# Seven products for eight on part of two more projections, their sums halved in two operations

## The chip, the core and the metric

The kernel runs on one core of a Trainium2 chip. TensorE (PE in the profile) multiplies, VectorE (DVE) and ScalarE (ACT) do elementwise work, GpSimd (POOL) a few small steps, and SyncE (SP) issues the loads. What is measured is the device time of one execution in microseconds (us).

## The reference

One decoder layer: 256 tokens, a model width of 2048, everything in float32.

```python
h = rms_norm(x, norm_g)
q, k, v, z_a, u_b, v_b, z_b, g_a, g_b = split(h @ w_in)   # seven of 1024 columns, two of 2048
att = moba_attention(rms_norm(q), rms_norm(k), v)         # 8 heads of 128
y_a = (att * silu(z_a)) @ w_proj_a                        # 1024 -> 2048
y_b = (spatial_gating(gelu(u_b), gelu(v_b)) * silu(z_b)) @ w_proj_b
merged = sigmoid(g_a) * y_a + sigmoid(g_b) * y_b
return x + merged @ w_out                                 # 2048 -> 2048
```

## The kernel before

**Units.** All weights are laid out on the host as a stream of 120 blocks of 128 x 2048 words (1 MB). Block i is a unit: one load into `raw{i}`, one preparation, one group of matmuls. The order of the units is that of `schedule()`: q (units 0 to 7), k (8 to 15), v, za, vb, ub and zb (48 to 55) of eight units each, then four times eight units of the gates (g0 to g3) followed by four of the two branch projections (`proj`), and last 16 units of the output projection (104 to 119). The eight units of a stage are the eight pairs kp = 0 to 7 of the contraction: each holds rows k and k + 8 (of 16 blocks of 128) for two blocks of 512 columns, so four blocks W11, W12, W21, W22.

**Float32 by halves.** Each operand is cast to a shorter format (h) on ACT, and what the cast lost (l) is subtracted out on DVE (`halve`). A product is then three matmuls, l x h, h x h and h x l (`three`): in a unit done directly, `wh` is the cast of the block and `wl` the rest.

**Eight products or seven.** A unit done directly (`direct`) takes eight products, 24 matmuls of 128 x 512. A unit with kp in `SK` that is not of q takes seven (`seven`, Winograd's form of Strassen's scheme), 21 matmuls, and is here called a seven unit. It needs four sums of weight blocks (`t`, three DVE operations), the halves of three blocks (`whp`, `wlp`, 1536 wide) and of the four sums (`th`, `tl`, 2048 wide), and forms of the other operand (`forms`, `halves_f`), made once. Its products go to three banks of PSUM that the direct units share (`L`) and four banks of their own (`E`). After the last seven unit of a stage `early` takes the E banks out, and after the last unit `final` adds the L banks.

**Buffers and order.** `raw` and `t` share four buffers, `wh` with `th` three, `wl` with `tl` three, `whp` and `wlp` two each. The preparation of unit i + 2 and the load of unit i + 3 are written at unit i, and a scheduler sets the order on each engine once the q stage is through. Every engine runs its instructions in that order. A table (`at`) adds the rest of the layer at given units; `turn_m` transposes column block c of the merged result (two transposes of four blocks into PSUM, then its halves) for the output projection, which is done directly, row by row of its columns (`mm_rows`, then `post_out`).

Of the kernel before, what the change touches and what calls it, by code (L numbers as in the profile page):

```python
# [46 lines left out]
def schedule():  # L47
    s = []

    def quad(name, c, order):  # L50
        s.extend(("quad", name, c, kp, n) for n, kp in enumerate(order))

    quad("q", 0, PLAIN)
    for name in ("k", "v", "za", "vb", "ub", "zb"):
        quad(name, 0, MIXED)
    for c in range(4):
        quad("g", c, MIXED)
        s.extend(("proj", "proj", c, q, q) for q in range(4))
    for c in range(4):
        s.extend(("out", "out", c, q, q) for q in range(4))  # L60
    return s
# [3 lines left out]
def hybrid_layer_kernel(  # L65
# [57 lines left out]
    def split(i, pieces=1, js=None):  # L123
# [119 lines left out]
    Fs, Fh, Fl = None, None, None  # L243
# [39 lines left out]
    def direct(L, hs, ls, i, kp, start, stop):  # L283
# [5 lines left out]
        for c, kh in order:  # L289
# [4 lines left out]
            three(L[c], hi, lo, wh[i][:, o:o + B], wl[i][:, o:o + B], start and kh == 0, stop and kh == 1,  # L294
                  first=(i == 0))

    def seven(E, L, i, kp, first, last, started):
# [3 lines left out]
        def A(kh, r):  # L301
            return xh[0][:, a + kh, r * P:(r + 1) * P], xl[0][:, a + kh, r * P:(r + 1) * P]

        def Fm(n):
            return Fh[:, n, kp % 4, :], Fl[:, n, kp % 4, :]
# [14 lines left out]
    def early(E, name):  # L320
# [160 lines left out]
    def turn_m(c, banks):  # L481
        t = slot(F32R, f"mT{c}").rearrange("p (a k t) -> p a k t", a=2, t=S)
        X["mT", c] = t
        for m in range(2):
            ps = transpose4(banks[m], X["m", c][m], f"ps_mT{c}{m}")
            halves(t[:, 0, :, m * P:(m + 1) * P], t[:, 1, :, m * P:(m + 1) * P], ps)
# [23 lines left out]
    def load_res(c):  # L510
        for m in range(2):
            xres[c, m] = u(f"xres{c}{m}")
            nc.scalar.dma_start(xres[c, m], x[m * P:(m + 1) * P, c * B:(c + 1) * B])

    def post_out(c, m, acc):
        o = xres[c, m]
        pieces = 2 if (c, m) == (3, 1) else 1
        n = B // pieces
        for a in range(pieces):
            sl = slice(a * n, (a + 1) * n)  # L520
            nc.vector.tensor_tensor(o[:, sl], acc[:, sl], o[:, sl], op=ALU.add)
            nc.sync.dma_start(out[m * P:(m + 1) * P, c * B + a * n:c * B + (a + 1) * n], o[:, sl])
# [72 lines left out]
    for kp in range(1, 4):  # L595
        split_x(kp)
        if kp < 2:
            split(kp, 4)
    E, L = [0, 2, 4, 3], [1, 5, 6, 7]
    e = None  # L600
    for i, (kind, name, c, kp, n) in enumerate(G):
# [8 lines left out]
        if kind == "quad":  # L610
            if n == 0:
# [7 lines left out]
            if kp in SK and not plain:
                seven(Et, Lt, i, kp, kp == SK[0], kp == SK[-1], n > 0)  # L620
                if kp == SK[-1]:
                    e = early(Et, f"{name}{c}")
            else:
                direct(Lt, xu_h if plain else xh, xu_l if plain else xl, i, kp, n == 0, n == 7)
# [100 lines left out]
```

## Time and profile before

| | |
|---|---|
| median of 3 runs | 681.86 us (681.32 to 682.17) |
| the profiled execution | 681.6 us, of which 679.8 us are the span of the profile |
| PE busy | 663.5 us (98%), 3018 matmuls and transposes |
| DVE busy | 554.6 us (82%) |
| ACT busy | 390.7 us (57%) |
| DMA | 135.31 MB, 199 GB/s |

Busy shares are means over stages that differ: the stage windows and the waits show where an engine is short. A matmul's duration in the profile overlaps the next one's; the distance of their starts is what one costs.

### The profile page before, as it was taken

The numbers are of one execution on the slowest core, as the hardware profiler recorded it, in microseconds if no ns is written. First come the engines' busy times: TensorE is split into PE (matmuls) and PEld (weight loads), VectorE is DVE, ScalarE is ACT, GpSimd is POOL, SyncE is SP. The second block draws the span as 40 slices with busy tenths as digits, with TensorE's granted clock in tenths as the row PEclk, the third lists the DMA queues.
The fourth block names the chain that finished last, engine by engine and source line by source line (L and its number), as shares of the span: only waits on it lengthen the run. The fifth ranks groups of instructions, "written<-read, shape, count | busy, mean of one in ns | idle before, by whom it ended". The sixth has DMA issues, their size and how long they took to land.

```text
span 679.8 us, 7696 instructions
## 1 busy us (share of the span) xinstructions
PE 663.5 (98%) x3018; PEld 544.1 (80%) x3018; DVE 554.6 (82%) x504; ACT 390.7 (57%) x459; POOL 33.3 (5%) x28
## 2 busy tenths in 40 slices
PE   8899999999999999999989999999999999999997
PEld 4677778788788887887877888888888888888886
DVE  4499988899999899998998988978879886654551
ACT  7777867766873685675545834654554555333330
POOL 1001203000010008000000000000000000000000
PEclk9999999999999999999999999999999999999999
DMA  8972573454444624734555725935763475846610
GB/s 305 419 254 79 185 272 142 153 239 168 193 166 186 245 74 177 288 132 161 224 182 224 275 75 200 338 129 185 269 227 124 186 287 211 272 179 235 232 39 31
DMA packets 21923, 135.31 MB, mean 199 GB/s; under 512 B 2432, under 2 KB 3072, under 8 KB 6656
## 3 DMA queue, kind: packets, MB, share of 16 engines
q1 hardware_dynamic: 20736, 132.73, 53.0%
q10 hardware_dynamic: 1152, 2.10, 1.2%
q8 instruction: 23, 0.38, 0.2%
q14 instruction: 12, 0.10, 0.0%
HBM read 132.72 MB, written 2.10 MB: 198 GB/s over the span
## 4 chain that ended last, share of the span: by engine, by line
PE 73%; DVE 12%; issue 4%; DMA 4%; ACT 4%; POOL 0%; SPq 0%; DVEq 0%; ACTq 0%
PE acc_g L279 14%; PE y L279 13%; PE acc_out L279 13%; PE seven_g L279 5%; PE acc_ub L279 4%; PE acc_za L279 4%; DMA raw<-in_w 4%; PE acc_vb L279 4%; DVE wl L121 3%; PE acc_v L279 2%; PE acc_zb L279 2%; DVE wlp L121 2%; ACT th L120 2%; DVE tl L121 2%; PE seven_za L279 2%
## 5 line engine op out<-in xcount | busy, mean ns | idle before, releaser
L121 DVE TENSOR_TENSOR wl<-raw,wh 128x2048 fp32r<-128x2048 f32 (+2 forms) x87 | 183.1, 2115 | 65.3 <-ACT wh L120 64.8
L120 ACT CAST wh<-raw 128x2048 fp32r<-128x2048 f32 (+2 forms) x87 | 153.7, 1774 | 103.3 <-PE acc_out L279 45.7
L120 ACT CAST th<-t 128x2048 fp32r<-128x2048 f32 x40 | 76.5, 1912 | 102.6 <-DVE t L141 102.6
L121 DVE TENSOR_TENSOR tl<-t,th 128x2048 fp32r<-128x2048 f32 x40 | 92.0, 2300 | 28.3 <-ACT th L120 27.7
L279 PE MATMUL acc_out<-wh,mT 128*128 128x512 f32 x256 | 79.0, 390 | 0.0
L120 ACT CAST whp<-raw 128x1536 fp32r<-128x1536 f32 x40 | 59.2, 1481 | 30.5 <-DMA raw<-in_w 16.1
L121 DVE TENSOR_TENSOR wlp<-raw,whp 128x1536 fp32r<-128x1536 f32 x40 | 70.0, 1751 | 0.5 <-ACT whp L120 0.5
L279 PEld LDWEIGHTS acc_out<-wh,mT 128*128 128x128 f32 x256 | 47.9, 188 | 9.8
L279 PE MATMUL acc_g<-wh,xh 128*128 128x512 f32 x128 | 49.8, 389 | 0.0
L279 PE MATMUL acc_out<-wl,mT 128*128 128x512 f32 x128 | 49.8, 389 | 0.0
L279 PE MATMUL acc_g<-wh,xl 128*128 128x512 f32 x128 | 49.7, 389 | 0.0
L138 DVE TENSOR_TENSOR t<-raw 128x1024 f32<-128x1024 f32 x40 | 48.8, 1219 | 0.6
L279 PE MATMUL acc_g<-wl,xh 128*128 128x512 f32 x128 | 48.9, 389 | 0.0
L229 POOL TENSOR_TENSOR rs<-ms,mhalf 128x4 f32<-128x4 f32 x12 | 25.8, 2171 | 126.2 <-DVE ms L228 126.2
L279 PE MATMUL acc_q<-wl,xuh 128*128 128x512 f32 x64 | 25.5, 399 | 3.1 <-DVE wl L121 2.9
L279 PEld LDWEIGHTS acc_g<-wl,xh 128*128 128x128 f32 x128 | 24.0, 188 | 5.2
L279 PEld LDWEIGHTS acc_g<-wh,xl 128*128 128x128 f32 x128 | 24.0, 188 | 5.0
L279 PEld LDWEIGHTS acc_out<-wl,mT 128*128 128x128 f32 x128 | 24.0, 188 | 5.0
L140 DVE TENSOR_TENSOR t<-t,raw 128x512 f32<-128x512 f32 x40 | 27.7, 693 | 0.3
L279 PEld LDWEIGHTS acc_g<-wh,xh 128*128 128x128 f32 x128 | 24.0, 188 | 5.0
L141 DVE TENSOR_TENSOR t<-t,raw 128x512 f32<-128x512 f32 x40 | 27.4, 684 | 0.3
L279 PE MATMUL acc_q<-wh,xuh 128*128 128x512 f32 x64 | 25.1, 392 | 1.6 <-ACT wh L120 1.6
(453 smaller groups left out, 1430.3 us busy)
## 6 DMA issues: line engine op xcount, KB each, us to landing
raw<-in_w SPq DMA_DIRECT2D x117, 1024.0 KB, 4.9
raw<-in_w SPq DMA_DIRECT2D x5, 512.0 KB, 7.4
xnat<-in_x SPq DMA_DIRECT2D x2, 1024.0 KB, 12.7
xres<-in_x ACTq DMA_DIRECT2D x8, 256.0 KB, 6.1
out<-xres SPq DMA_DIRECT2D x7, 256.0 KB, 4.6
xt<-in_xT SPq DMA_DIRECT2D x3, 512.0 KB, 9.6
raw<-in_w SPq DMA_DIRECT2D x2, 256.0 KB, 4.7
ws<-in_wsT SPq DMA_DIRECT2D x2, 256.0 KB, 3.0
```

What stands on the lines that cost most here:

```text
L120: nc.scalar.copy(h, r)
L121: nc.vector.tensor_tensor(l, r, f(h), op=ALU.subtract)
L138: nc.vector.tensor_tensor(two, r[:, B:3 * B].rearrange("p (a n) -> p a n", a=2), r[:, None, 0:B].to_broadcast([P, 2, B]), op=ALU.add)
L140: nc.vector.tensor_tensor(t[:, 2 * B:3 * B], t[:, 0:B], r[:, 2 * B:3 * B], op=ALU.add)
L141: nc.vector.tensor_tensor(t[:, 3 * B:], t[:, 2 * B:3 * B], r[:, 3 * B:], op=ALU.add)
L229: nc.gpsimd.tensor_tensor(dst, ms[:, :n], mhalf[:, :n], op=ALU.pow)
L279: nc.tensor.matmul(acc, a, b, start=(start and n == 0), stop=(stop and n == 2))
```

## The change

Four things change.

- Each of the four gate stages does a fifth pair, kp = 4, with seven products (5 of 8). The forms for this pair are 128 wide (`forms_4`), and their halves are put into columns of `xh[0]` and `xl[0]` that no seven unit reads (`halves_4`). The order of the pairs becomes `GATE`.
- The output projection becomes two stages of eight pairs (out0 and out1, 1024 columns each) with pairs 0 to 3 in seven products. The merged result is kept in float32 too (`mf`), its forms are made while the last branch projection runs (`forms`, `halves_f` with "m"), and `turn_m` 2 comes ahead of 1. The residual x is added in `early` instead of at the end.
- The halves of the four sums are made in two operations each on ACT and DVE (columns 0 to 1023, then the rest), and the casts stand ahead of the subtractions.
- The seven products come in the order W21, W22, W11, sums 0, 1, 2, 3. Before it was W21, W22, sum 3, W11, sums 2, 1, 0.

```diff
+GATE = (5, 0, 1, 6, 2, 3, 4, 7)
+OUT = ((0, 1, 4, 2, 5, 3, 6, 7), (4, 0, 1, 5, 2, 3, 6, 7))
...
-        quad("g", c, MIXED)
+        quad("g", c, GATE)
...
-    for c in range(4):
-        s.extend(("out", "out", c, q, q) for q in range(4))
+    for c in range(2):
+        quad("out", c, OUT[c])
...
+        return G[i][3] in SK or (G[i][1] == "g" and G[i][3] == 4)
...
-        halve(wh[i], wl[i], r[:, B:])
...
-        halve(th[i], tl[i], t)
+        a, b = slice(0, 2 * B), slice(2 * B, WORDS)
+        nc.scalar.copy(wh[i], r[:, B:])
+        for sl in (a, b):
+            nc.scalar.copy(th[i][:, sl], t[:, sl])
+        nc.vector.tensor_tensor(wl[i], r[:, B:], f(wh[i]), op=ALU.subtract)
+        for sl in (a, b):
+            nc.vector.tensor_tensor(tl[i][:, sl], t[:, sl], f(th[i][:, sl]), op=ALU.subtract)
...
-        for acc, (hi, lo), (bh, bl) in ((L[0], A(1, 0), W("21")), (L[1], Fm(3), W("22")), (L[2], A(1, 1), T(3))):
-            three(acc, hi, lo, bh, bl, not started, False)
-        for acc, (hi, lo), (bh, bl) in ((E[0], A(0, 0), W("11")), (E[1], Fm(1), T(2)), (E[2], Fm(2), T(1)),
-                                       (E[3], Fm(0), T(0))):
-            three(acc, hi, lo, bh, bl, first, last)
+        for acc, (hi, lo), (bh, bl) in ((L[0], A(1, 0), W("21")), (L[1], Fm(3), W("22")), (E[0], A(0, 0), W("11")),
+                                       (E[3], Fm(0), T(0)), (E[2], Fm(2), T(1)), (E[1], Fm(1), T(2)),
+                                       (L[2], A(1, 1), T(3))):
+            three(acc, hi, lo, bh, bl, first if any(acc is e for e in E) else not started, last and any(acc is e for e in E))
...
+        if res:
+            for t, r, op in ((c11, res[0], ALU.add), (c12, res[1], ALU.subtract), (h, res[2], ALU.add),
+                             (c22, res[3], ALU.subtract)):
+                nc.vector.tensor_tensor(t, t, r, op=op)
...
+    at(i0 + 4, forms_4)
+    at(i0 + 5, lambda: forms(xt[0], "x"))
...
+    at(i0 + 20, halves_4)
...
-    at(first["proj", 3] + 1, turn_m, 1, "L23")
-    at(first["proj", 3] + 3, turn_m, 2, "L23")
-    at(first["out", 0] + 1, turn_m, 3, "L23")
-    for c in range(4):
-        at(first["out", 0] + 4 * c - 2, load_res, c)
+    at(first["proj", 3] + 1, turn_m, 2, "L23")
+    at(first["proj", 3] + 2, lambda: forms(X["mf", 0], "m"))
+    at(first["proj", 3] + 2, halves_f, "m")
+    at(first["proj", 3] + 2, turn_m, 1, "L01")
+    at(first["out", 0] + 0, turn_m, 3, "L3")
+    at(first["out", 0] + 0, load_res, 0)
+    at(first["out", 1] - 1, load_res, 1)
```

What this does to the order of the engines, at three places. First PE in a seven unit of the gates (g1; `xh`, `xl`, `Fh`, `Fl` are the other operand's halves). Before, unit 70 up to the first matmul that reads `tl`:

```order
L279 MATMUL acc_g1_0_3093<-whp70_3085,xl0_419 128x512
L279 MATMUL acc_g1_0_3093<-whp70_3085,xh0_418 128x512
L279 MATMUL acc_g1_0_3093<-wlp70_3086,xh0_418 128x512
L279 MATMUL acc_g1_1_3094<-whp70_3085,Fl_423 128x512
L279 MATMUL acc_g1_1_3094<-whp70_3085,Fh_422 128x512
L279 MATMUL acc_g1_1_3094<-wlp70_3086,Fh_422 128x512
L279 MATMUL acc_g1_2_3095<-th70_3089,xl0_419 128x512
L279 MATMUL acc_g1_2_3095<-th70_3089,xh0_418 128x512
L279 MATMUL acc_g1_2_3095<-tl70_3090,xh0_418 128x512
```

Now, unit 72 up to the same point:

```order
L303 MATMUL acc_g1_0_3175<-whp72_3240,xl0_424 128x512
L303 MATMUL acc_g1_0_3175<-whp72_3240,xh0_423 128x512
L303 MATMUL acc_g1_0_3175<-wlp72_3241,xh0_423 128x512
L303 MATMUL acc_g1_1_3176<-whp72_3240,Flx_428 128x512
L303 MATMUL acc_g1_1_3176<-whp72_3240,Fhx_427 128x512
L303 MATMUL acc_g1_1_3176<-wlp72_3241,Fhx_427 128x512
L303 MATMUL seven_g1_0_3209<-whp72_3240,xl0_424 128x512
L303 MATMUL seven_g1_0_3209<-whp72_3240,xh0_423 128x512
L303 MATMUL seven_g1_0_3209<-wlp72_3241,xh0_423 128x512
L303 MATMUL seven_g1_3_3212<-th72_3242,Flx_428 128x512
L303 MATMUL seven_g1_3_3212<-th72_3242,Fhx_427 128x512
L303 MATMUL seven_g1_3_3212<-tl72_3243,Fhx_427 128x512
```

The first use of the low half of the sums moves from the ninth matmul to the twelfth, and only its first 1024 columns are read there; the last columns are first read by the 18th.

Second DVE near the end of g0 (units 61 to 63; `t` sums, `wlp` and `tl` low halves). Before, where 61 and 62 are the last two seven units of the stage:

```order
L121 TENSOR_TENSOR wl60_2713<-raw60_2668,wh60_2712 128x2048
L138 TENSOR_TENSOR t61_2747<-raw61_2710 128x1024
L121 TENSOR_TENSOR wlp61_2752<-raw61_2710,whp61_2751 128x1536
L140 TENSOR_TENSOR t61_2747<-t61_2747,raw61_2710 128x512
L121 TENSOR_TENSOR wlp62_2787<-raw62_2745,whp62_2786 128x1536
L141 TENSOR_TENSOR t61_2747<-t61_2747,raw61_2710 128x512
L138 TENSOR_TENSOR t62_2782<-raw62_2745 128x1024
L140 TENSOR_TENSOR t62_2782<-t62_2782,raw62_2745 128x512
L121 TENSOR_TENSOR tl61_2756<-t61_2747,th61_2755 128x2048
L141 TENSOR_TENSOR t62_2782<-t62_2782,raw62_2745 128x512
L121 TENSOR_TENSOR tl62_2791<-t62_2782,th62_2790 128x2048
L121 TENSOR_TENSOR wl63_2821<-raw63_2780,wh63_2820 128x2048
```

Now, where they are the last two of three in a row (60 precedes them in the same form):

```order
L143 TENSOR_TENSOR t61_2813<-raw61_2770 128x1024
L155 TENSOR_TENSOR wlp61_2818<-raw61_2770,whp61_2817 128x1536
L145 TENSOR_TENSOR t61_2813<-t61_2813,raw61_2770 128x512
L157 TENSOR_TENSOR tl61_2820<-t61_2813,th61_2819 128x1024
L146 TENSOR_TENSOR t61_2813<-t61_2813,raw61_2770 128x512
L155 TENSOR_TENSOR wlp62_2858<-raw62_2811,whp62_2857 128x1536
L157 TENSOR_TENSOR tl61_2820<-t61_2813,th61_2819 128x1024
L143 TENSOR_TENSOR t62_2853<-raw62_2811 128x1024
L145 TENSOR_TENSOR t62_2853<-t62_2853,raw62_2811 128x512
L146 TENSOR_TENSOR t62_2853<-t62_2853,raw62_2811 128x512
L157 TENSOR_TENSOR tl62_2860<-t62_2853,th62_2859 128x1024
L126 TENSOR_TENSOR wl63_2891<-raw63_2851,wh63_2890 128x2048
```

Each `tl` stands in two pieces, the first of them right behind the second sum and not behind the third; the last piece of `tl62` follows `wl63`.

Third DVE between the last branch projection (units 100 to 103) and the output projection (`ps_mT` transposed blocks, `g3` the last gate, `y` the branch projections). Before:

```order
L121 TENSOR_TENSOR wl104_4289<-raw104_4226,wh104_4288 128x2048
L471 TENSOR_TENSOR mT0_4256<-ps_mT00_4257,mT0_4256 128x4x128
L471 TENSOR_TENSOR mT0_4256<-ps_mT01_4264,mT0_4256 128x4x128
L471 TENSOR_TENSOR mT1_4271<-ps_mT10_4272,mT1_4271 128x4x128
L471 TENSOR_TENSOR mT1_4271<-ps_mT11_4279,mT1_4271 128x4x128
L121 TENSOR_TENSOR wl105_4325<-raw105_4286,wh105_4324 128x2048
L494 TENSOR_TENSOR g3_c12_4150<-y2_30_4292,g3_c12_4150 128x512
L494 TENSOR_TENSOR g3_c22_4149<-y2_31_4293,g3_c22_4149 128x512
L495 TENSOR_TENSOR g3_c11_4147<-g3_c11_4147,g3_c12_4150 128x512
L495 TENSOR_TENSOR g3_h_4148<-g3_h_4148,g3_c22_4149 128x512
L121 TENSOR_TENSOR wl106_4376<-raw106_4322,wh106_4375 128x2048
```

Now, from the third form of the merged result on:

```order
L289 TENSOR_TENSOR Fm_4446<-mf0_4373,Fm_4446 128x512
L145 TENSOR_TENSOR t105_4473<-t105_4473,raw105_4404 128x512
L157 TENSOR_TENSOR tl105_4480<-t105_4473,th105_4479 128x1024
L146 TENSOR_TENSOR t105_4473<-t105_4473,raw105_4404 128x512
L531 TENSOR_TENSOR g3_c11_4262<-y0_30_4315,g3_c11_4262 128x512
L295 TENSOR_TENSOR Flm_4452<-Fm_4446,Fhm_4451 128x2048
L502 TENSOR_TENSOR ml1_4456<-ps_mT10_4457,mh1_4455 128x4x128
L502 TENSOR_TENSOR ml1_4456<-ps_mT11_4464,mh1_4455 128x4x128
L157 TENSOR_TENSOR tl105_4480<-t105_4473,th105_4479 128x1024
L531 TENSOR_TENSOR g3_h_4263<-y0_31_4316,g3_h_4263 128x512
L533 TENSOR_TENSOR g3_c12_4265<-y2_30_4420,g3_c12_4265 128x512
L533 TENSOR_TENSOR g3_c22_4264<-y2_31_4421,g3_c22_4264 128x512
```

Ahead of the last two merges there now stand the sums and the low halves of units 104 and 105, the forms of the merged result and their low half `Flm`; before there stood two `wl`.

## Rows read from the trace of the kernel before

**Rows 1.** The page: busy time by engine, then the clock in 40 slices.

```profile
PE 663.5 (98%) x3018; PEld 544.1 (80%) x3018; DVE 554.6 (82%) x504; ACT 390.7 (57%) x459; POOL 33.3 (5%) x28
...
PEclk9999999999999999999999999999999999999999
```

**Rows 2.** Chain that ended last, in order of time: start, us, what.

```profile
563.65 10.88 PE y L279 x48
574.53 1.75 PE ps_mT L376 x16
...
587.22 0.87 PE ps_mT L376 x8
...
676.05 0.02 issue
```

**Rows 3.** Stage windows: v, zb, g0, g2, its projection, the last projection, output projection.

```profile
core 0: us, PE busy (x) PEld busy (x) DVE busy (x) ACT busy (x) POOL busy (x), PEclk, DMA share, GB/s
99.16:143.23 44.07, 43.20 (x198) 35.23 (x196) 38.63 (x37) 33.76 (x66) 6.21 (x7) 1.00 0.52 191
283.60:328.84 45.24, 44.73 (x213) 37.19 (x212) 41.53 (x37) 28.66 (x34) 0.00 (x0) 1.00 0.50 191
328.84:374.14 45.30, 41.99 (x182) 33.61 (x181) 41.62 (x37) 24.12 (x19) 0.00 (x0) 1.00 0.50 184
460.29:501.09 40.80, 40.80 (x182) 33.80 (x181) 35.26 (x31) 19.56 (x13) 0.00 (x0) 1.00 0.59 229
501.09:522.85 21.76, 21.76 (x98) 18.02 (x97) 17.32 (x14) 11.95 (x9) 0.00 (x0) 1.00 0.43 148
563.65:588.09 24.44, 24.44 (x122) 20.55 (x121) 15.70 (x16) 12.09 (x12) 0.00 (x0) 1.00 0.71 226
588.09:676.05 87.96, 87.95 (x392) 72.58 (x391) 40.26 (x27) 27.64 (x18) 0.00 (x0) 1.00 0.46 161
```

**Rows 4.** PE in time, in v and in g0: start, us, [idle before <- what ended it].

```profile
118.42 0.39 PE L279 MATMUL seven_v<-whp,xl 128*128 128x512 f32 x1
119.67 0.50 PE L279 MATMUL acc_v<-tl,xh 128*128 128x512 f32 x1 [0.87 <-DVE tl L121]
...
365.60 0.50 PE L279 MATMUL acc_g<-th,xl 128*128 128x512 f32 x1 [1.40 <-ACT th L120]
```

**Rows 5.** DVE in time, zb and g0, columns as in group 4.

```profile
289.22 1.21 DVE L138 TENSOR_TENSOR t<-raw 128x1024 f32<-128x1024 f32 x1
290.36 1.75 DVE L121 TENSOR_TENSOR wlp<-raw,whp 128x1536 fp32r<-128x1536 f32 x1
292.02 0.68 DVE L140 TENSOR_TENSOR t<-t,raw 128x512 f32<-128x512 f32 x1
292.63 1.75 DVE L121 TENSOR_TENSOR wlp<-raw,whp 128x1536 fp32r<-128x1536 f32 x1
...
303.36 2.29 DVE L121 TENSOR_TENSOR tl<-t,th 128x2048 fp32r<-128x2048 f32 x1 [1.43 <-ACT th L120]
...
365.57 2.29 DVE L121 TENSOR_TENSOR tl<-t,th 128x2048 fp32r<-128x2048 f32 x1 [2.02 <-ACT th L120]
367.78 2.29 DVE L121 TENSOR_TENSOR wl<-raw,wh 128x2048 fp32r<-128x2048 f32 x1
...
564.21 0.68 DVE L335 TENSOR_TENSOR g_c<-acc_g,g_c 128x512 f32<-128x512 f32 x1
```

**Rows 6.** Groups by form: busy, mean ns of one, idle before.

```profile
L365 DVE SCALAR_TENSOR_TENSOR vb_c<-vb_c,rs,gain 128x128 f32<-128x128 f32 x12 | 3.3, 345 | 0.0
L470 ACT CAST mT<-ps_mT 128x512 fp32r<-128x512 f32 x8 | 4.2, 593 | 0.0
L120 ACT CAST wh<-raw 128x1024 fp32r<-128x1024 f32 x2 | 2.0, 1047 | 0.0
L120 ACT CAST th<-t 128x2048 fp32r<-128x2048 f32 x40 | 76.5, 1912 | 102.6 <-DVE t L141 102.6
```

**Rows 7.** Loads by line: KB each, median us from issue to landing.

```profile
raw<-in_w SPq DMA_DIRECT2D x117, 1024.0 KB, 4.9
```

More of the change, by code (lines that the diff above doesn't have):

```diff
@@ L293, in direct, with seven @@
             o = BLK[f"{kh + 1}{col + 1}"] * B
-            three(L[c], hi, lo, wh[i][:, o:o + B], wl[i][:, o:o + B], start and kh == 0, stop and kh == 1,
+            three(L[c], hi, lo, wh[i][:, o:o + B], wl[i][:, o:o + B], start[c == 3] and kh == 0, stop and kh == 1,
                   first=(i == 0))
-    def seven(E, L, i, kp, first, last, started):
+    def seven(E, L, i, kp, first, last, started, hs, ls, Fh, Fl):
         a = 2 * (kp % 4)
         def A(kh, r):
-            return xh[0][:, a + kh, r * P:(r + 1) * P], xl[0][:, a + kh, r * P:(r + 1) * P]
+            return hs[kp // 4][:, a + kh, r * P:(r + 1) * P], ls[kp // 4][:, a + kh, r * P:(r + 1) * P]
         def Fm(n):
-            return Fh[:, n, kp % 4, :], Fl[:, n, kp % 4, :]
+            if kp == 4:
+                return spare(hs[0])[:, n], spare(ls[0])[:, n]
+            return Fh[:, n, kp, :], Fl[:, n, kp, :]
         def W(b):
@@ L481, in turn_m @@
     def turn_m(c, banks):
-        t = slot(F32R, f"mT{c}").rearrange("p (a k t) -> p a k t", a=2, t=S)
-        X["mT", c] = t
+        i = c % 2
+        for a in ("mh", "ml") + (("mf",) if i == 0 else ()):
+            if (a, i) not in X:
+                X[a, i] = slot(F32 if a == "mf" else F32R, f"{a}{i}").rearrange("p (k t) -> p k t", t=S)
         for m in range(2):
-            ps = transpose4(banks[m], X["m", c][m], f"ps_mT{c}{m}")
-            halves(t[:, 0, :, m * P:(m + 1) * P], t[:, 1, :, m * P:(m + 1) * P], ps)
+            ps = transpose4(banks[m % len(banks)], X["m", c][m], f"ps_mT{c}{m}")
+            d = (slice(None), slice(c // 2, 8, 2), slice(m * P, (m + 1) * P))
+            if i == 0:
+                nc.scalar.copy(X["mf", i][d], ps)
+            if i == 0 and c == 0 and m == 1:
+                continue
+            halves(X["mh", i][d], X["ml", i][d], ps)
     def merge(c, Y):
@@ L510, in load_res, with post_out @@
     def load_res(c):
[L511 to L522, printed above, removed]
+        xres[c] = [u(f"xres{c}{j}") for j in range(4)]
+        for j, t in enumerate(xres[c]):
+            m, o = j // 2, (2 * c + j % 2) * B
+            nc.scalar.dma_start(t, x[m * P:(m + 1) * P, o:o + B])
+    def post_out(c, L, e):
+        for j in range(4):
+            m, o = j // 2, (2 * c + j % 2) * B
+            pieces = 2 if (c, j) == (1, 3) else 1
+            n = B // pieces
+            for a in range(pieces):
+                sl = slice(a * n, (a + 1) * n)
+                final_one(L, e, j, sl)
+                nc.sync.dma_start(out[m * P:(m + 1) * P, o + a * n:o + (a + 1) * n], e[j][:, sl])
     first = {}
@@ L598, in hybrid_layer_kernel, with fac, direct22 @@
             split(kp, 4)
+    def fac(name):
+        if name == "q":
+            return xu_h, xu_l
+        if name == "out":
+            return [X.get(("mh", i)) for i in range(2)], [X.get(("ml", i)) for i in range(2)]
+        return xh, xl
+    def direct22(i):
+        return any(not strassen(j) for j in range(i - G[i][4], i))
     E, L = [0, 2, 4, 3], [1, 5, 6, 7]
@@ L614, in hybrid_layer_kernel @@
                     E, L = L, E
-                Lt = [bank(b, f"acc_{name}{c}_{j}") for j, b in enumerate(L)]
+                Lt = [bank(b, f"acc_{name}{c}_{j}") for j, b in enumerate(L[:3])]
                 Et = None
-            if not plain and kp in SK and Et is None:
+            if len(Lt) == 3 and (plain or not strassen(i)):
+                Lt.append(bank(L[3], f"acc_{name}{c}_3"))
+            if strassen(i) and Et is None:
                 Et = [bank(b, f"seven_{name}{c}_{j}") for j, b in enumerate(E)]
[L619 to L622, printed above, removed]
+            if strassen(i):
+                last = 4 if name == "g" else SK[-1]
+                f8 = "m" if name == "out" else "x"
+                seven(Et, Lt, i, kp, kp == SK[0], kp == last, n > 0, *fac(name), X["Fh", f8], X["Fl", f8])
+                if kp == last:
+                    e = early(Et, f"{name}{c}", xres.get(c) if name == "out" else None)
             else:
-                direct(Lt, xu_h if plain else xh, xu_l if plain else xl, i, kp, n == 0, n == 7)
+                direct(Lt, *fac(name), i, kp, (n == 0, not direct22(i)), n == 7)
             if n == 7:
@@ L629, in hybrid_layer_kernel @@
                         nc.scalar.activation(X[name][j // 2][j % 2], Lt[j], AF.Copy, scale=rstd[:, j // 2:j // 2 + 1])
+                elif name == "out":
+                    post_out(c, Lt, e)
                 elif name == "g":
@@ L677, in hybrid_layer_kernel @@
                     a[-1] = L[2:4]
+                elif a[-1] == "L3":
+                    a[-1] = L[3:4]
             fn(*a)
```

70 lines of the change are left out of this document (35 added, 35 removed).

## The prediction

> **What bounds the kernel now.** I read the page first, then the chain of waits, then windows cut at the stages, and last PE and DVE in time. [...] No term of the sum is a clock. In the chain the last third is PE alone: 48 matmuls take 10.88 us [rows 2], so one costs 0.2267 us, a unit of 24 takes 5.44 us and one of 21 takes 4.76 us, 0.68 us less. A stage of four and four is then 40.80 us, and g2 takes exactly that [rows 3]: from g1 on PE waits for nothing, and each matmul taken out there is worth its price, if what feeds PE keeps up.
>
> Before g1 that is not so. g0 takes 45.30 us for the same work [rows 3], 4.50 us of waits. v takes 44.07, of which 40.80 are products and 1.75 are 16 transposes (as many as the ps_mT of [rows 2]): 1.5 us of waits. zb has 0.5 us that PE is not busy [rows 3]. The two waits shown are PE waiting for `tl` and for `th` [rows 4], the halves of the sums. Behind them stands DVE. In zb and g0 it is idle ahead of a `tl` four times, 1.4 to 2.05 us at a time and 6.94 us in all (the first and the last stand in [rows 5]), each time until ACT has cast all 2048 columns, and ACT itself had sat waiting for the third sum (102.6 us in all, [rows 6]). Otherwise DVE is full there.
>
> **The matmuls.** Twelve more units are done in seven products, four in the gates and eight in the output projection. 12 x 0.68 = 8.16 us leave PE. Of that 0.68 lie in g0, 2.04 in g1 to g3 and 5.44 in the output projection.
>
> **What DVE gets for it.** Taken by the distance of starts in [rows 5], a 1024 wide sum costs 1.14 us, a 512 wide operation 0.60, a 1536 wide low half 1.66, a 2048 wide one 2.21. A direct unit costs DVE 2.21. A seven unit cost 1.14 + 0.60 + 0.60 + 1.66 + 2.21 = 6.21, and costs 6.28 with its last step in two pieces of 1.14. Twelve units turned add some 49 us to DVE and the 40 older ones 3 us. A block of gates and projection (g2) has 62.56 us of PE time and 52.6 us of DVE work [rows 3]; it becomes 61.88 and 57.0. In the output projection 40.3 us of 87.96 [rows 3] become about 74 of 82.5 (six of its eight seven units are prepared inside it, and 24 operations of `early` and `final` replace nine). So DVE still fits, but within a gate stage itself, without its projection, it is over PE: 35.3 + 4.4 = 39.7 us plus its waits against 40.1. It has to work ahead during the projections and carry that lead in three buffers.
>
> **What the two halves and the new order give.** The first cast needs only the first sum; in the order of DVE the first piece of `tl` stands behind the second sum, and PE asks for it at the twelfth matmul and for the last piece at the 18th instead of for everything at the ninth: 0.7 and 2.0 us later. An ACT cast of 1024 columns takes 1.05 us where the whole takes 1.91 [rows 6], so the wait of 2 us in [rows 5] should close: while the piece is cast, a sum or a `wlp` runs. I take v's 1.5 us as gone.
>
> In g0 DVE decides. Before, it ran from the first sum of unit 50 at 289.22 to the end of the last `tl` of g0 at 367.78 [rows 5], 78.56 us: by the order that is 8 x 6.21 + 5 x 2.21 + 16 x 0.60 = 70.3 of work, 6.94 of waits for `th`, 1.3 of small gaps between dependent operations. Now the same stretch holds 9 x 6.28 + 5 x 2.21 + 16 x 0.60 = 77.2, and the 1.3. It begins 1.5 us earlier, since v gave that back: 287.7 + 78.5 = 366.2. Behind the last piece of `tl62` 19 matmuls are left in PE's order, 4.3 us: g0 ends at 370.5 and not at 374.14, **3.6 us earlier**. The ends of this term: if DVE gates nothing, g0 ends 1.5 + 0.5 + 4.5 + 0.68 = 7.2 us earlier; if the waits of 6.94 stay, 3.3 us later. I take the middle figure, because the waits' cause is taken away and the added unit is counted.
>
> [...]
>
> **The start of the output projection.** Here DVE gets in 24 us what it had no part of: the sums and halves of units 104 and 105, four forms, their low half, and the residue of the blocks turned. By the order, from `wl102` to the low half of block 1, which frees the bank of out0's first shared product, it is 3 x 2.21 + 2 x 1.14 + 2 x 1.66 + 3 x 1.14 + 13 x 0.60 = 23.5 us. Before, the last `final` of g3 ended 1.2 us after the projection began (564.21 + 0.68 against 563.65, [rows 5] and [rows 2]). With one more seven unit in g3 I take 4.6, because the load of unit 100 waits for a buffer until the added unit's `wlp` is done. DVE is then there at 28.1 us. PE is there at 21.76 + 2.62 (24 transposes, [rows 2]) + 1.13 (five matmuls placed ahead) = 25.5. **2.6 us of waiting.** If the finals come as early as before it is 0. If DVE also keeps its 8.7 us of idle time of that stretch (24.44 - 15.70, [rows 3]), it is 11.3. I stay at 2.6: that idle time was waiting for buffers with nothing else to do. The last two merges follow 3.5 us later, and PE reaches their banks by then, since the products that need them are the last of its order.
>
> **The rest.** Where out0 meets out1, `early`, the residual and `final` are 12 operations of 0.60, and the load of unit 116 stands in SP's queue behind four stores of out0, the last of which waits for the last `final`. I put 0.5 us for the low half of the unit before it, between 0 and 4.9, one whole load uncovered [rows 7]. The forms of pair 4 are four 128 wide operations, between 0 and 4 x 0.345 = 1.4 us [rows 6], in the middle of DVE's work at the end of q; I put 0, as unit 10 now asks for its low halves later than they come; without that cover it is the 1.4. The four copies into `mf` cost ACT 4 x 0.59 [rows 6] in a stretch where it is idle half the time [rows 3]; the casts in two pieces cost it 2 x 1.05 - 1.91 = 0.18 us each, hidden as it is busy 57%. The tail behind the last matmul (679.8 - 676.05 = 3.75 us, [rows 2]) has the same two half stores at its end: 0. Loads are the same bytes.
>
> **The sum.** 681.6 for the profiled execution (0.3 below the median of the runs), - 3.6 up to the end of g0, - 2.04, - 5.44, + 2.6, + 0.5: **673.6 us.**
>
> **Rivals.**
> - *All waits go.* DVE's lead covers g0 and the start of out0 too. Then 681.6 - 8.16 - 4.5 - 1.5 - 0.5 = 666.9 us. For it: the casts come earlier at every unit. Against it: DVE's count in zb and g0 leaves no slack at all. 0.14.
> - *The start of out0 costs most of the gain.* DVE is late by 6 to 11 us, as its bound above: 677 to 682. For it: bank and merges hang on DVE's order, in which the sums stand first. 0.15.
> - *DVE becomes the bound of the gates (slower).* Place: g1 to g3. In g2 and its projection DVE is idle 9.98 us now [rows 3], waiting for `wh` until PE frees a buffer. If those waits stay where they are and the added 4.4 comes on top, a block takes 57.0 + 9.98 = 67.0 against 61.9, 5.1 us each and 15 us for three: 689 us. It decides from 2.7 us a block on. Against it: the idle time lies ahead of `wl` with spare time in the projections, and the pieces shorten it. 0.07.
> - *The change does not do what it says:* excluded, as the order of PE has 36 matmuls fewer and twelve seven units more.
>
> **How the numbers follow.** My forecast, with all its terms near their middle, has 0.64 (669 to 678). A measurement here can tell 0.2%, 1.4 us. The chance of faster is 0.64, 0.14 and most of the second rival: 0.87; of no difference 0.05, from the second; of slower 0.08, from the third and the second's end. The range that leaves out 2 in 10 runs from 666.5 to 679.
>
> **What would show it.** Right, step by step: 5.44 and 4.76 us a unit unchanged; v near 42.6 us; no idle DVE of 1.4 to 2 us ahead of a `tl` in zb and g0; g1 to g3 at 40.12; a wait of some 3 us of PE for DVE at the first products of out0, and 81.6 us plus little from there on. Wrong, if g1 to g3 are longer than 40.8, if g0 still waits 4 us or none, or if out0 waits for a merge or a load.

## The result and the profile after

The changed kernel takes **671.94 us** in the median of four executions (669.00 to 674.05), the kernel before 681.8 us (681.32 to 682.17): a ratio of 0.9853, 95% interval 0.9813 to 0.9893. The forecast was 673.6 us. The profiled execution took 670.06 us, its span 668.3. Of ten executions of this kernel, these four and the six of a later series, five lay at 673.8 us or more and five at 671.2 or less; the experiments show why.

The page of the changed kernel, busy time by engine and the clock:

```profile
PE 655.2 (98%) x2982; PEld 539.5 (81%) x2982; DVE 617.3 (92%) x629; ACT 418.1 (63%) x530; POOL 29.3 (4%) x28
...
PEclk9999999999999999999999999999999999999999
```

PE has 36 matmuls fewer than in [rows 1] and 8.3 us less to do, DVE 62.7 us more, the clock is the same. The stages, as in [rows 3] (v, zb, g0, g2, its projection, the last projection, output projection):

```profile
98.51:141.78 43.27, 42.89 (x197) 35.41 (x196) 40.77 (x44) 33.04 (x69) 9.02 (x7) 1.00 0.52 195
281.95:326.36 44.41, 44.41 (x213) 37.36 (x212) 43.34 (x46) 29.07 (x39) 0.00 (x0) 1.00 0.52 190
326.36:369.44 43.08, 41.28 (x179) 33.06 (x178) 42.03 (x41) 24.97 (x22) 0.00 (x0) 1.00 0.48 179
454.91:495.03 40.12, 40.12 (x179) 33.23 (x178) 37.15 (x36) 21.44 (x18) 0.00 (x0) 1.00 0.65 235
495.03:516.79 21.76, 21.76 (x98) 18.02 (x97) 19.16 (x17) 12.23 (x11) 0.00 (x0) 1.00 0.42 148
556.91:581.37 24.46, 24.46 (x122) 20.56 (x121) 23.98 (x25) 18.30 (x22) 0.00 (x0) 1.00 0.53 185
581.37:664.26 82.89, 82.86 (x368) 67.92 (x367) 77.17 (x78) 37.92 (x30) 0.00 (x0) 1.00 0.51 180
```

g2 is at exactly 40.12 and the output projection at 82.89, of which 81.6 us are counted as products. In g0, 43.08 stand against 40.12. In the last projection DVE is busy 23.98 of 24.46 us, and PE loses nothing. The groups of the sums' halves, as in [rows 6]:

```profile
L154 ACT CAST th<-t 128x1024 fp32r<-128x1024 f32 x104 | 109.3, 1053 | 119.4 <-DVE t L143 53.7
...
L157 DVE TENSOR_TENSOR tl<-t,th 128x1024 fp32r<-128x1024 f32 x104 | 126.1, 1216 | 5.2 <-ACT th L154 5.2
```

DVE stands idle ahead of a `tl` for 5.2 us in the whole run, where it was 28.3 with 40 units.

Each stage, from its first product to that of the next (PE in time), in the profiled executions (the windows above run to the end of a stage's last product, 0.16 us after the next stage's first has started); the columns after the first two are experiments below, the last of them with four units in seven products in g0:

| us | before | changed | sevens alone | pieces, old order | no added sevens | no power on POOL |
|---|---|---|---|---|---|---|
| start to v | 99.16 | 98.51 | 98.94 | 98.62 | 99.83 | 98.99 |
| v | 44.07 | 43.27 | 44.76 | 43.40 | 44.21 | 42.64 |
| za, vb, ub | 140.37 | 140.17 | 141.71 | 140.20 | 141.71 | 139.43 |
| zb | 45.24 | 44.41 | 45.06 | 44.39 | 44.42 | 44.55 |
| g0 | 45.14 | 42.92 | 48.27 | 42.34 | 41.13 | 40.80 |
| g1 to g3, three projections | 189.51 | 187.47 | 187.77 | 187.82 | 189.91 | 188.02 |
| last projection | 24.35 | 24.46 | 24.46 | 24.42 | 24.36 | 24.42 |
| output projection | 87.81 | 82.66 | 85.41 | 82.73 | 87.80 | 82.70 |
| behind the last product | 4.15 | 4.43 | 4.82 | 4.18 | 4.13 | 4.15 |
| span | 679.8 | 668.3 | 681.2 | 668.1 | 677.5 | 665.7 |

### The profile page after: what moved, and what is told of

Its sections match the earlier page's. It is cut to its first block, busy times and chain, and to the rows that moved or that the text cites. A ratio compares the mean times of both kernels' runs of the same rounds, so it can differ in the third digit from the quotient of the medians.

```text
span 668.3 us, 7843 instructions
## 1 busy us (share of the span) xinstructions
PE 655.2 (98%) x2982; PEld 539.5 (81%) x2982; DVE 617.3 (92%) x629; ACT 418.1 (63%) x530; POOL 29.3 (4%) x28
## 4 chain that ended last, share of the span: by engine, by line
PE 65%; DVE 17%; ACT 6%; issue 6%; DMA 5%; POOL 1%; SPq 0%; DVEq 0%; ACTq 0%
PE y L303 13%; PE acc_g L303 13%; PE acc_out L303 9%; PE seven_g L303 6%; DMA raw<-in_w 5%; PE acc_ub L303 5%; PE acc_vb L303 4%; DVE tl L157 3%; PE seven_out L303 3%; DVE wl L126 3%; PE acc_za L303 3%; DVE t L143 2%; ACT wh L125 2%; DVE wlp L155 2%; PE seven_vb L303 2%
## 5 line engine op out<-in xcount | busy, mean ns | idle before, releaser
L154 ACT CAST th<-t 128x1024 fp32r<-128x1024 f32 x104 | 109.3, 1053 | 119.4 <-DVE t L143 53.7
L126 DVE TENSOR_TENSOR wl<-raw,wh 128x2048 fp32r<-128x2048 f32 (+2 forms) x75 | 156.0, 2087 | 24.4 <-ACT wh L125 24.2
L157 DVE TENSOR_TENSOR tl<-t,th 128x1024 fp32r<-128x1024 f32 x104 | 126.1, 1216 | 5.2 <-ACT th L154 5.2
L303 PE MATMUL acc_q<-wl,xuh 128*128 128x512 f32 x64 | 25.6, 400 | 2.7 <-DVE wl L126 2.7
L303 PE MATMUL acc_q<-wh,xul 128*128 128x512 f32 x64 | 25.8, 403 | 0.6 <-ACT wh L125 0.6
L303 PE MATMUL y<-wh,zbl 128*128 128x512 f32 x64 | 25.1, 392 | 0.0
L303 PE MATMUL y<-wh,zah 128*128 128x512 f32 x64 | 25.0, 391 | 0.0
L303 PE MATMUL y<-wh,zal 128*128 128x512 f32 x64 | 25.0, 391 | 0.0
L303 PE MATMUL y<-wl,zbh 128*128 128x512 f32 x64 | 24.9, 389 | 0.0
L303 PE MATMUL y<-wh,zbh 128*128 128x512 f32 x64 | 24.9, 389 | 0.0
L303 PE MATMUL y<-wl,zah 128*128 128x512 f32 x64 | 24.9, 389 | 0.0
```

Source lines behind the costliest of these rows:

```text
L126: nc.vector.tensor_tensor(l, r, f(h), op=ALU.subtract)
L154: nc.scalar.copy(th[i][:, sl], t[:, sl])
L157: nc.vector.tensor_tensor(tl[i][:, sl], t[:, sl], f(th[i][:, sl]), op=ALU.subtract)
L303: nc.tensor.matmul(acc, a, b, start=(start and n == 0), stop=(stop and n == 2))
```

## The experiments

Theory: DVE decides up to the end of g0 and at the start of out0, and the pieces with the new order take its waits away. The rivals are that the 36 matmuls are the whole gain, and that DVE comes to bound the gates.

**The added units alone.** Sums halved whole, products in the old order.

```diff
-        for sl in (a, b):
-            nc.scalar.copy(th[i][:, sl], t[:, sl])
...
+        halve(wh[i], wl[i], r[:, B:])
+        halve(th[i], tl[i], t)
...
-        for acc, (hi, lo), (bh, bl) in ((L[0], A(1, 0), W("21")), (L[1], Fm(3), W("22")), (E[0], A(0, 0), W("11")),
+        for acc, (hi, lo), (bh, bl) in ((L[0], A(1, 0), W("21")), (L[1], Fm(3), W("22")), (L[2], A(1, 1), T(3)),
```

> The changed kernel with the sums halved whole and the products in the old order: the twelve added units in seven products alone. Theory (DVE decides up to the end of g0, and the halves in two pieces with the new order take its waits away): the waits of v (1.5 us) and g0 (4.5 us) stay and the fifth unit of g0 brings another 4 us of DVE work and a wait of 1.5 us or more, so the gates' first products of the projection come 3 us later than in the kernel before instead of 4.7 us earlier, and the start of out0 waits some us: 680 to 686 us. Rival 1 (the pieces and the order are worth nothing; all gain is the 36 matmuls taken out): 672 to 674 us. Rival 2 (DVE becomes the bound of the gates g1 to g3): 689 us, g1 to g3 each longer than 42 us.

Measured: 683.56 us (682.94 to 684.22), ratio 1.0026 (1.0017 to 1.0035). With the same 36 matmuls fewer the kernel is 1.8 us slower than before, as theory has it. g0 takes 3.1 us more than before and the output projection gives 2.4 of its 5.4 us; in both PE waits for the cast of a whole sum. za to ub take 1.3 us more. PE's waits, groups (us in total, times, longest):

```profile
PE acc_g L298 <- ACT th L125: 4.4, 2, 2.9
...
PE acc_out L298 <- ACT th L125: 1.8, 2, 1.4
```

g1 in a window of its own:

```profile
402.80:442.91 40.11, 40.11 (x178) 33.21 (x178) 38.84 (x34) 20.93 (x14) 0.00 (x0) 1.00 0.62 236
```

So DVE does not bound the gates behind g0 even without the pieces, and the 36 matmuls alone are no gain: both rivals fall.

**The new order, sums halved whole.** The first half of the diff above.

> The changed kernel with the sums halved whole again, the new order of products kept. Theory: PE asks for the sums' halves at the tenth matmul of a unit and not at the seventh (one product, 0.68 us later), but each tl still waits for a cast of 1.9 us: DVE idles 1.4 to 2 us ahead of a tl again in zb and g0, and the time lies 3 to 7 us above the changed kernel, 675 to 679 us. Rival (the order is what takes the waits away, the pieces nothing): 671 to 673 us.

Measured: 683.98 us (683.18 to 685.42), ratio 1.0035 (1.0023 to 1.0046), no better than with the old order. Both theory and rival missed: the order alone gives nothing.

**Two pieces, the old order.** The second half of that diff.

> The changed kernel with the products in the old order, the sums still halved in two pieces. The old order asks for the last sum in its third product, so for the second piece of tl at the ninth matmul. Theory: DVE has no idle time ahead of tl, so where DVE decides (g0, start of out0) only the demand comes nine matmuls, 2 us, earlier once at the end of each stretch in which DVE decides: 2 to 4 us above the changed kernel, 674 to 676 us. Rival (pieces alone give it, the order nothing): 671 to 673 us.

Measured: 670.03 us (669.92 to 670.16), ratio 0.9825 (0.9810 to 0.9839). Nearest to the rival, and 1 us below its range: the pieces give all that pieces and order give together, and these four executions lie with the shorter ones of the changed kernel. Its profile shows a reason why the written order is worth so little. PE in time near the end of g0:

```profile
358.17 0.50 PE L303 MATMUL seven_g<-tl,Fhx 128*128 128x512 f32 x1
358.51 0.39 PE L303 MATMUL acc_g<-tl,xh 128*128 128x512 f32 x1
360.38 0.50 PE L303 MATMUL seven_g<-th,xl 128*128 128x512 f32 x1 [1.48 <-ACT th L154]
360.71 0.39 PE L303 MATMUL seven_g<-th,xh 128*128 128x512 f32 x1
360.95 0.40 PE L303 MATMUL seven_g<-th,xl 128*128 128x512 f32 x1
361.18 0.39 PE L303 MATMUL seven_g<-th,xh 128*128 128x512 f32 x1
361.89 0.50 PE L303 MATMUL seven_g<-tl,xh 128*128 128x512 f32 x1 [0.32 <-DVE tl L157]
```

The code writes a product as two matmuls with `th` and then one with `tl`; here two products have their `th` matmuls first. The scheduler sets PE's order, and in the kernel with the old order, too, these two products have their `th` matmuls first (360.06 to 360.86 us there). So where PE waits, both kernels run much the same order whatever the code writes; that this is the whole reason is argued, not shown.

**Pieces and order without the added units.** The kernel before with the new halving and the new order.

> The kernel before with the halving in two pieces and the new order of products, and no unit more in seven products. Theory: v gives back 1.5 us, zb 0.5, g0 3.5 to 4.5 of its 4.5 us of waits, nothing from g1 on: 675.3 to 676.5 us. Rival (all gain is the 36 matmuls): 681.8 us, as before.

Measured: 678.35 us (677.88 to 679.26), ratio 0.9944 (0.9928 to 0.9961): 3.4 us, not the 5.3 to 6.5 expected. g0 gives 4.0 as expected, but v gives nothing, and za to ub take 1.3 us more. That is read from the profiled execution (table), the longest of its four: in v ACT waited 5.0 us for POOL (see the repeat of the changed kernel), and in za PE waited 1.3 us for DVE ahead of the attention scores. So the parts do not add: the units alone cost 1.8 us, the other two parts alone give 3.4, and all together 9.9.

**Casts in two pieces, the low half in one.** Old order.

```diff
-        for sl in (a, b):
-            nc.vector.tensor_tensor(tl[i][:, sl], t[:, sl], f(th[i][:, sl]), op=ALU.subtract)
+        nc.vector.tensor_tensor(tl[i], t, f(th[i]), op=ALU.subtract)
```

> Old order of products; ACT casts the sums in two pieces of 1024 columns, but DVE takes their low half whole, in one operation of 2048. Theory (what counts is that DVE does not stand idle while ACT casts): ACT has half the cast behind the third sum, so DVE's idle time ahead of tl falls from 27.6 us to some 10 us or less, and DVE does 0.07 us less per unit: 671 to 675 us. Rival 1 (the two pieces of tl are needed, since a whole tl stands behind the second cast): 678 to 683 us, near the whole halving. Rival 2 (the pieces of tl give nothing): 669.5 to 670.5 us.

Measured: 677.75 us (677.3 to 678.2), ratio 0.9940 (0.9924 to 0.9957), nearest to the first rival; theory, by which DVE's idle time counts and would fall, missed. Of DVE's groups, and of PE's waits:

```profile
L156 DVE TENSOR_TENSOR tl<-t,th 128x2048 fp32r<-128x2048 f32 x52 | 119.0, 2289 | 28.1 <-ACT th L154 28.0
...
PE acc_g L302 <- ACT th L154: 0.4, 1, 0.4
```

The idle time is that of the whole halving, since a whole `tl` still stands behind the cast of the third sum. Of the 13.5 us between whole and pieces, the casts alone give 5.8. What fell with them is not DVE's idle time but PE's waits for `th` in g0 and in the output projection, 4.4 and 1.8 us with whole casts, here 0.4 and none. The rest takes `tl` in pieces. The casts' pieces came with the casts' place ahead of the subtractions, and no run separates the two.

**The changed kernel again.**

> The changed kernel once more, beside the other kernels of this group, because its four runs lay between 669.0 and 674.05 us while the kernel with the old order of products lay between 669.9 and 670.2. Theory (the written order of products gives nothing; where PE waits, the program's own scheduling already puts products whose operands are there ahead): 669 to 671 us here, less than 0.3% from the old order. Rival (the new order costs something in part of the executions): some executions at 673.5 to 674 us again.

Measured: 672.52 us (668.56 to 675.29), ratio 0.9855 (0.9824 to 0.9886). The rival: the spread is there again. The profiled execution took 674.05 us, and only one stage differs by more than 0.4 us from the first profile: v took 46.83 us, not 43.27. POOL in time in v, in the first profile of the changed kernel (670.06 us):

```profile
114.09 2.13 POOL L239 TENSOR_TENSOR rs<-ms,mhalf 128x4 f32<-128x4 f32 x1 [36.91 <-DVE ms L238]
```

ACT in time, the same profile:

```profile
116.25 0.99 ACT L388 ACTIVATE k_c<-k_c,rs 128x128 f32<-128x128 f32 x3 [2.19 <-POOL rs L239]
117.15 1.47 ACT L152 CAST whp<-raw 128x1536 fp32r<-128x1536 f32 x1
```

POOL in the longer execution:

```profile
114.44 5.46 POOL L239 TENSOR_TENSOR rs<-ms,mhalf 128x4 f32<-128x4 f32 x1 [37.13 <-DVE ms L238]
```

ACT in the longer execution:

```profile
119.93 0.99 ACT L388 ACTIVATE k_c<-k_c,rs 128x128 f32<-128x128 f32 x3 [5.54 <-POOL rs L239]
120.83 1.46 ACT L152 CAST whp<-raw 128x1536 fp32r<-128x1536 f32 x1
```

DVE in the longer execution:

```profile
114.48 1.21 DVE L157 TENSOR_TENSOR tl<-t,th 128x1024 fp32r<-128x1024 f32 x1
115.62 2.28 DVE L126 TENSOR_TENSOR wl<-raw,wh 128x2048 fp32r<-128x2048 f32 x1
117.82 1.21 DVE L143 TENSOR_TENSOR t<-raw 128x1024 f32<-128x1024 f32 x1
122.32 1.76 DVE L155 TENSOR_TENSOR wlp<-raw,whp 128x1536 fp32r<-128x1536 f32 x1 [3.29 <-ACT whp L152]
```

`rs` is the power of -1/2 for k's norms (`rsqrt`). It took 3.3 us longer; ACT waited for it with the cast of a unit queued behind, and DVE stood idle 3.29 us behind that cast. v was 3.6 us longer.

**Four units in seven products in g0.** Two pieces, old order.

```diff
-        quad("g", c, GATE)
+        quad("g", c, MIXED if c in (0,) else GATE)
```

> Two pieces, old order of products, and four instead of five units in seven products in g0 alone (g1 to g3 keep five). Theory (DVE decides g0): DVE has 6.28 - 2.21 = 4.1 us less to do there, PE 0.68 more, and the 2.0 us that PE still waits for th and tl in g0 go; g0 takes 40.8 to 41.2 us where it took 42.3: 668.5 to 669.2 us. Rival (the waits left in g0 are loads, not DVE's count): g0 stays at 42.3 us or longer, 670.0 to 670.7 us.

Measured: 669.59 us (668.58 to 673.38), ratio 0.9835 (0.9810 to 0.9859); the median does not tell it from 670.03, and two of its six executions took 673.2 us or more. The profiled execution does: g0 took 40.80 us, all of it products, where it took 42.34. With 4.1 us of DVE work fewer and 0.68 us of PE work more the stage is 1.5 us shorter, so DVE decides g0.

**The residue's low half twice.**

```diff
-        nc.vector.tensor_tensor(Fl, X["F", name], f(Fh), op=ALU.subtract)
+        for _ in range(2 if name == "m" else 1):
+            nc.vector.tensor_tensor(Fl, X["F", name], f(Fh), op=ALU.subtract)
```

> Two pieces, old order, and the low half of the residue's four forms computed twice (the same result written again): one more 2048 wide DVE operation, 2.21 us, in p3, ahead of the low half that frees the bank of out0's first shared product. Theory (DVE and PE come to that bank within 0.3 us of each other, DVE last): out0's waits grow by 2.0 to 2.4 us, 672.0 to 672.4 us. Rival (DVE has slack there, the 0.2 us wait is a bank or a semaphore): less than 0.7 us, 670.0 to 670.7 us.

Measured: 670.32 us (670.12 to 671.78), ratio 0.9838 (0.9818 to 0.9858). It says nothing on the question: the second operation (582.55 us) came to stand behind the low half that frees the bank (581.95). It shows that 2.2 us more of DVE work inside out0 are hidden.

**Four more forms ahead of out0.**

```diff
-        nc.vector.tensor_tensor(F[2], a11, a21, op=ALU.subtract)
+        for _ in range(5 if Fs.shape[2] == 4 and src is not xt[0] else 1):
+            nc.vector.tensor_tensor(F[2], a11, a21, op=ALU.subtract)
```

> Two pieces, old order, and one of the residue's four forms computed five times (the same result written again): four more 512 wide DVE operations in p3, 4 x 0.60 = 2.4 us, which this time stand ahead of the low half that frees the bank of out0's first shared product; in the run before, one such addition came to stand behind it. Theory (DVE and PE come to that bank within 0.3 us of each other, DVE last): the first products of out0 wait 1.8 to 2.4 us more, 671.8 to 672.6 us if nothing gives it back. Rival (DVE has slack there): less than 0.7 us, 670.0 to 670.7 us.

Measured: 672.21 us (670.83 to 673.62), ratio 0.9856 (0.9840 to 0.9872), two of its four executions at 673.37 and 673.62. The median lies in theory's range by those two, which is luck: the short ones are 0.8 to 1.0 us above 670.03, between theory and rival. In the profiled one (670.83) the output projection took 83.71 us against 82.73. PE of that kernel, at the bank:

```profile
583.64 0.39 PE L304 MATMUL seven_out<-wlp,mh 128*128 128x512 f32 x1
584.71 0.50 PE L304 MATMUL acc_out<-whp,ml 128*128 128x512 f32 x1 [0.69 <-DVE ml L503]
```

DVE freed the bank 2.2 us later than in the changed kernel (584.7 against 582.5), as theory has it, but PE lost 1.0 us: six more matmuls had been put ahead, 11 where there were five. DVE is last there, and the scheduling hides more than half of its lateness.

**A pair of operations on POOL ahead of k's powers.** On the changed kernel.

```diff
+        nc.gpsimd.tensor_tensor(d, c[:, 0:4], c[:, 0:4], op=ALU.mult)
+        nc.gpsimd.tensor_tensor(d, d, mhalf[:, 0:4], op=ALU.pow)
```

> The changed kernel, with two small operations of 128x4 on POOL (a product and a power, of k's first columns, their result used by nobody) ahead of the four powers that k's norms need. In a longer execution of the changed kernel the first of these four powers took 5.46 us, in a shorter one 2.13, ACT waited for it with the cast of a unit queued behind, and v took 46.8 and 43.3 us. Theory (the first power after POOL has rested is the slow one, and its length makes the spread): the extra pair takes the delay ahead of time, and all executions lie between 668.5 and 670.6 us. Rival 1 (any power may be slow, at random): a spread to 674 us remains, with a later power of the four, or the first, long in it. Rival 2 (the spread comes from elsewhere, loads for one): it remains, and v is not what differs.

Measured: 675.15 us (670.47 to 675.84), ratio 0.9890 (0.9869 to 0.9911). The theory fell: the added power took 1.01 us though POOL had done nothing for 22.6 us up to the pair, and the first `rs`, 13 us later, took 5.46 us again. It is not a matter of POOL having rested. Five executions of six took 675.06 us or more; the profiled one is among them.

**The same pair, with g0 at four.**

> The same pair on POOL, with the old order of products, two pieces, and four units in seven products in g0. Theory: both gains add up, since one lies in v and one in g0: 668.5 to 669.5 us in every execution, median 0.5 to 1.5 us below the old order with five. Rival: the median stays at 669.6 to 670.1 us, with executions at 673 us.

Measured: 669.11 us (668.53 to 675.56), ratio 0.9808 (0.9796 to 0.9821), with two of seven executions at 673 or more: the median is where theory has it, the spread is the rival's. The profiled one (675.56) has a first `rs` of 5.46 us, so the pair does not take it away here either.

**No power on POOL.** Two pieces, old order, g0 at four, no extra pair.

```diff
-        nc.gpsimd.tensor_tensor(dst, ms[:, :n], mhalf[:, :n], op=ALU.pow)
+        nc.scalar.activation(ms[:, :n], ms[:, :n], AF.Sqrt)
+        nc.vector.reciprocal(dst, ms[:, :n])
```

> Two pieces, old order, four units in seven products in g0, no extra pair on POOL; and the norms' power of -1/2 no longer on POOL but as a square root on ACT (128x4 each) and a reciprocal on DVE. Theory (in the long executions the first power on POOL ends 0.9 us behind the end of a DVE instruction and 5.46 us behind its own start, so POOL gets its operands only between two DVE instructions and now and then misses several such places; ACT and the unit's cast stand behind it): without POOL in that chain no execution is long; all within 1.5 us of each other, 668 to 670 us. Rival (the spread of v comes from something else, or ACT's change of function costs as much as the power): executions at 673 us or more remain, or all lie above 670.5 us.

Measured: **667.95 us** (667.51 to 668.30), ratio 0.9792 (0.9779 to 0.9806), the best of all and the narrowest spread with g0 at four. v and g0 in windows:

```profile
98.99:141.63 42.64, 42.64 (x197) 35.34 (x196) 41.23 (x48) 34.79 (x75) 1.96 (x3) 1.00 0.54 204
325.61:366.57 40.96, 40.96 (x182) 33.94 (x181) 39.90 (x38) 23.74 (x22) 0.00 (x0) 1.00 0.58 206
```

PE is busy all through v, which is 0.6 to 0.8 us shorter than with either order of products, and no execution is long. The wait for POOL was what was left there. That it also made the spread rests on the profiles of the kernels with pieces and the added units: the three executions at 674 us or more have a first `rs` of 5.46 us, the five between 668.9 and 670.9 us one of 1.01 or 2.13. Five executions without a long one are few as evidence, since with POOL and g0 at four 4 of 13 were long. ACT's order moved with the edit (the unit's cast now stands ahead of k's scaling, not behind its first three), so it is not told apart whether POOL's absence or that place does more; both belong to the one wait.

## Why the prediction was right, and where not

The forecast summed to 8.0 us of gain; the profiled executions differ by 11.5 us in span, the medians by 9.9. That the median, 671.94, lies so near 673.6 is in part luck. The five shorter executions lie 2.4 to 5.0 us below the forecast, in the profiled one mostly because the wait at out0 did not come; the five longer ones come up to it by a wait for POOL that no term has.

- **The matmuls.** Right: g1 to g3 took 40.12 us each, 0.68 us less, and the stretch from g1 to the last projection 189.51 - 187.47 = 2.04.
- **Up to the end of g0**, forecast 3.6, measured 4.7. That DVE decides g0 is borne out by the run with four units there, but not at the place that was forecast. DVE ended the last piece of `tl62` at 365.59 us, forecast 366.2, and 16 matmuls stood behind it and not 19; yet PE did not wait for it. PE ran without a break from 361.89 on. Its last waits are the two in the rows above, 1.48 us for the first cast of unit 62, which waited for the first sum of that unit on DVE, and 0.32 for the first piece of `tl62`. The start was right by luck: zb began 1.65 us earlier, forecast 1.5, but v gave 0.80 of it and the stretch ahead of v, which is in no term, 0.65. Rows of DVE in the changed kernel, a piece and that first sum, and the last piece of `tl62`:

```profile
356.89 1.22 DVE L157 TENSOR_TENSOR tl<-t,th 128x1024 fp32r<-128x1024 f32 x1
358.03 1.22 DVE L143 TENSOR_TENSOR t<-raw 128x1024 f32<-128x1024 f32 x1
...
364.37 1.22 DVE L157 TENSOR_TENSOR tl<-t,th 128x1024 fp32r<-128x1024 f32 x1
```

  A piece costs 1.14 us as reckoned, so two cost 0.07 more than one whole (2.21 in [rows 5]).
- **v's waits gone** was wrong in its cause. I put the 1.5 us down to the cast of whole sums. In the changed kernel 0.7 us were left (43.27 against 40.80 + 1.75), in the longer execution 3.6 us came on top, and all went only when no cast stood behind a wait for POOL. In the kernel before, too, ACT had waited 3.42 us for `rs` there, with the cast of a whole sum behind it. ACT of that kernel:

```profile
114.80 0.70 ACT L357 ACTIVATE k_c<-k_c,rs 128x128 f32<-128x128 f32 x2 [3.42 <-POOL rs L229]
115.40 1.90 ACT L120 CAST th<-t 128x2048 fp32r<-128x2048 f32 x1
```

  POOL's own first power is 1.46 us of this wait; it began when DVE had made its operand, at 113.31. The step named the cast and had not read what stands ahead of it in ACT's queue.
- **The new order** was reckoned to put off PE's demand by 0.7 and 2.0 us. It gave nothing that the runs show: 670.03 without it. The step took the written order for PE's order where PE waits.
- **The start of out0**, forecast a wait of 2.6 us, measured 0.2 us at that bank; the last projection took 0.11 us more. This is the term that was mis-sized most. PE of the changed kernel at the bank, the last matmul ahead of it and the first that needs it:

```profile
582.11 0.39 PE L303 MATMUL acc_out<-th,mh 128*128 128x512 f32 x1
582.52 0.50 PE L303 MATMUL acc_out<-whp,ml 128*128 128x512 f32 x1
```

  The 23.5 us for DVE's chain held: from the end of g3's last `final`, 1.5 us after the projection began, to the bank at 582.5 are 24.3 us. What failed was the 4.6 us taken for the finals. I let them be late by the added unit's load; they came 1.5 us after the projection's start, nearly as early as before (1.4 counted the same way, 1.2 in the forecast). PE came to that bank 25.6 us after the projection's start as forecast (25.5), and DVE 0.2 us later.
- **out0 to out1**, forecast 0.5 us: the output projection is 5.15 us shorter out of 5.44, and the 0.3 that are missing lie at that bank: the wait of 0.2 and a first matmul that takes 0.34 us and not 0.23. So nothing is left for this term. The tail took 0.28 us more, forecast 0.
- **The rivals.** "All waits go" (666.9) is what the last experiment nearly reaches, 668.0, by other means. "DVE becomes the bound of the gates" fell: 40.11 in g1 even without pieces.

## What to carry to other kernels

Removing work from the engine that is busy 98% paid nothing by itself (1.8 us lost) while the engine that feeds it stood idle behind a cast; cutting the cast and its consumer into pieces made the same removal worth its price. Where a scheduler orders an engine, the order written in the code is no evidence of the order in which operands are asked for. Before a wait is put down to the operation it names, read what stands ahead of that operation in its engine's queue.

## What the runs showed of the hardware

- **A small operation on POOL beside a full DVE.** In nine profiles of kernels with pieces, the first of k's four `rs` and DVE's next operation start within 0.32 us of each other, and how far POOL is ahead goes with its time:

| POOL ahead of DVE by, us | first `rs` takes, us | profiles |
|---|---|---|
| 0.32, 0.09, 0.08, 0.05 | 1.01 | old order; low half twice; four more forms; g0 four |
| 0.05 | 2.13 | changed kernel, first profile |
| 0.04, 0.04, 0.04, 0.03 | 5.46 | changed kernel again; pair on POOL; no added sevens; pair and g0 four |

  In the long ones it ended 0.86 to 0.87 us behind the end of the third DVE operation from there (119.03 and 119.90 in the rows above), after which DVE had nothing to do; in the 2.13 one behind the first (115.36 and 116.22). So it looks as if some hundredths of a us decided whether POOL gets through at once or stays out until a DVE operation ends, not always the next. Two profiles at 0.05 differ, and no run sets that distance on purpose: this is argued from nine profiles, not shown. By the recorded starts POOL was ahead in all nine, and in five of them its operation took 2.13 us or more, so which of the two starts first does not tell them apart. The trace does not show DVE losing anything (the `wl` of 2048 beside it took 2.28 us, as elsewhere). In three profiles with whole `tl` (the kernel before, the added units alone, the casts in two pieces) the first `rs` took 1.45 or 1.46 us, in the nine with pieces 1.01 to 5.46. In the kernel before, where DVE stood idle for 3.28 us beside them, k's four powers took 4.38 us together; in eight of the nine 5.48 to 9.93. So with fewer gaps on DVE POOL's part of the path grew less even, though the change does not touch POOL.
- **The granted clock fell after some waits.** PE of the run with the added units alone, in g0: it stood 2.85 us for a cast, and in the next 3.5 us the clock was 0.52. Windows of that kernel:

```profile
343.21:346.45 3.24, 0.39 (x2) 0.00 (x0) 3.00 (x6) 1.95 (x2) 0.00 (x0) 1.00 0.35 51
346.45:350.00 3.55, 3.55 (x9) 2.84 (x10) 3.55 (x2) 3.55 (x3) 0.00 (x0) 0.52 0.59 249
```

  Matmuls then started 0.42 us apart (347.05 and 347.47) and not 0.23, by an estimate some 1.4 us more for seven of them: this wait cost half as much again. It is a part of the 48.27 us of g0 there. The run with the pair on POOL has it in v of its profiled execution: PE stood 1.79 us for a `tl`, up to 139.95 us, and soon after the clock was 0.52:

```profile
140.52:143.41 2.89, 2.89 (x8) 2.21 (x7) 2.85 (x3) 1.90 (x1) 0.00 (x0) 0.52 0.94 391
```

  So the same 5.46 us on POOL cost unlike amounts: v took 46.83 us in the longer execution of the changed kernel, where the clock stayed at 1.00 though PE had stood 1.78 us for the same `tl`, 48.35 us here, and 49.83 us with the pair, the old order and g0 at four, where matmuls started 0.43 us apart from 139.88 to 142.87. The slower matmuls are a part of these differences.
